# Issuing 334 stores of a hybrid decoder layer from GpSimd's queue instead of SyncE's

## The chip, the cores and the metric

One core of one Trainium2 chip runs one launch of the kernel. The metric is device time in microseconds, the median of several runs. The engines are named as in the profile: PE (TensorE), DVE (VectorE), ACT (ScalarE), POOL (GpSimd) and SP (SyncE, which here does nothing but issue DMAs). All five run their own instruction streams in order and wait for each other through semaphores.

## The reference

One decoder layer in f32, for 1024 prompt tokens and 8 sample tokens (all 1032 columns pass through the same weights). Width 1024.

```
h = LN0(alpha*h + 0.5*swiglu(h; ffn1))
p = h @ w_in                        # RWKV r,k,v and low-rank parts; RG-LRU; GeLU; two gates
rwkv = rwkv7(shifted p, decay, a, gate via low-rank matrices)   # 16 heads x 64, chunked scan
lru  = rg_lru(conv4(p_lru)) * gelu(p_gelu)
h = LN1(alpha*h + (g0*rwkv + g1*lru) @ w_mix_out)
h = LN2(alpha*h + cross_attention(h; 4 heads, 256 memory tokens))
y = LN3(alpha*h + 0.5*swiglu(h; ffn2))
```

It also returns the memory's keys and values (`mk`, `mv`), the RWKV states (`prwkv`, `srwkv`), the last projection columns (`shift`), the last inputs of the convolution (`conv`) and the state of the RG-LRU (`lru`).

## The kernel before, in words

Activations lie transposed: 128 channels on the partitions, 1032 token columns in three chunks of 344 (or four of 256 and one of 8), and eight such blocks `k` for the width. `acc` holds the residual; `HH` and `HL` its high and low parts, since a product is made of three matmuls (`mm3`, L125 to L127: HH x wh, HL x wh, HH x wl). A weight tile of 128x512 is loaded by SP (L94), its high part made by ACT (L99) and its low part by DVE (L100); in the feed-forward parts the same is at L228 and L229, and POOL adds tiles there (L246, L334).

The stages in the order of the trace: feed-forward 1 (0 to 700 us); LN0 and the first columns of the projection (700 to 770); the low-rank part (770 to 880); the mixer (880 to 2000); output projection, LN1 and the memory's keys and values (2000 to 2150); attention (2150 to 2390); LN2 and the start of feed-forward 2 (2390 to 2470); feed-forward 2 with LN3 at its end.

A layer norm (`ln_stream`, L160 to L219) takes one chunk of columns at a time: the mean by a matmul with ones (L169); for each block `k` the subtraction of the mean on DVE (L181), the square on ACT (L183), and for each pair the sum on POOL (L185); the matmuls over the squares on PE (L176); DVE adds epsilon (L192), POOL raises to the power -1/2 (L193), ACT broadcasts (L195), PE transposes (L200); then for each block scale on DVE (L205), bias on ACT (L207), HH on ACT (L214), HL on POOL (L215), and, where the layer norm's result is needed later as a residual, a store of the block to DRAM (L217): `HD` behind LN0 (24 stores of 128x344), `H` behind LN2 (24 of 128x256 and 8 of 128x264).

The mixer writes the projected columns to a DRAM tile `GD`, one for each of eight pairs of heads, and reads them back when their turn comes. `project` (L635) makes one 128-row tile of it: gemm, evacuation on ACT (`ev`, L556), store to GD (L644). That store is issued from POOL for 150 of the 168 tiles, and from SP for the 18 in the low-rank part, where `then` is None. `ends` (L652) copies the last columns of a finished tile from GD to the outputs `shift` (L655) and `conv` (L657): these DMAs go from DRAM to DRAM and wait until the store to GD has landed. The low-rank part stores decay, `a` and gate to GD (L762, L763) and two output columns (L734). Each round of the mixer takes one pair and 256 columns: loads of GD tiles, RWKV chunks on PE, DVE and ACT, the RG-LRU, and the merge. In it, POOL raises to powers for norms (L798 in `inv_norm`, `ivs` and `ivc`, whose results ACT makes into `s` and `gsq` and PE transposes at L804; L1150 and L1220), copies `BN` (L894), and issues loads of `MG` (L1241) and stores of `FD` (L1257). The stores of the rounds are the bonus (L863), the LRU's state and output (L1041, L1046, L1050), the merged rows `MG` (L1084, L1229) and the RWKV states (L1138, L1198). `memory_kv` (L1372) stores each key and value tile twice, to a DRAM tile and to the output (L1396, L1397, L1412). Attention stores the sample queries and probabilities to small DRAM tiles (`qd` L1547, `pd` L1555), which loads read at once.

The program is written as generators that are woven together, and a scheduler then sets the order of each engine's instructions, so a change of an instruction's engine can change the order of others. DMAs are instructions in the stream of the engine that issues them and run in that stream's order. The line at the centre of the change in `project` was:

```
(nc.gpsimd if then else nc.sync).dma_start(out=GD[p][:, gi, c0:c0 + n], in_=e)
```

Of the kernel before, what the change touches and what calls it, by code (L numbers as in the profile page):

```python
# [159 lines left out]
def ln_stream(S, st, li, c0, n, final, keep):  # L160

    nc = S.nc
# [39 lines left out]
    for k in range(KT):  # L202
        d = acc[:, k, c0:c0 + n]
        g, b = S.lng[:, li, k:k + 1], S.lnb[:, li, k:k + 1]
        nc.vector.scalar_tensor_tensor(out=d, in0=d, scalar=g, in1=rs[:, :n], op0=ALU.mult, op1=ALU.mult)  # L205
        if final is None or k % 3 < 2:
            nc.scalar.activation(out=d, in_=d, func=AF.Identity, bias=b)  # L207
        else:
            nc.vector.tensor_scalar(out=d, in0=d, scalar1=b, scalar2=None, op0=ALU.add)  # L209
        if final is not None:  # L210
            nc.sync.dma_start(out=final[128 * k:128 * k + 128, c0:c0 + n], in_=d)
        else:
            hh = S.HH[:, k, c0:c0 + n]
            nc.scalar.activation(out=hh, in_=d, func=AF.Identity)  # L214
            nc.gpsimd.tensor_tensor(out=S.HL[:, k, c0:c0 + n], in0=d, in1=hh.bitcast(F32), op=ALU.subtract)  # L215
            if keep is not None:
                nc.sync.dma_start(out=keep[k, :, c0:c0 + n], in_=d)  # L217
        yield
# [325 lines left out]
def mixer(octx, S, I, O, MG, HD, pre):  # L544
# [13 lines left out]
    with ExitStack() as ctx:  # L558
# [76 lines left out]
        def project(p, mt, gi, func, sc, w, cs, psg, pool, then=None):  # L635

            for c0, n in cs:
                q = psg(n)
                yield from cols(w, c0, n, q)
                if then:  # L640
                    then(c0, n)
                e = pool.tile([128, 344], F32, tag="ev", name="ev", bufs=3 if then else 2)[:, :n]
                ACT(e, q, func, scale=sc)
                (nc.gpsimd if then else nc.sync).dma_start(out=GD[p][:, gi, c0:c0 + n], in_=e)  # L644

# [6 lines left out]
        def ends(p, early):  # L652

            for i in range(3 if early else 0):
                nc.sync.dma_start(out=O["shift"][:, 8 * i + p, :], in_=GD[p][:, i, NP - 1:NT])  # L655
            if not early:
                nc.sync.dma_start(out=O["conv"][:, p, :], in_=GD[p][:, GL, NP - 3:NT])  # L657

# [42 lines left out]
        with ExitStack() as c2:  # L701
# [25 lines left out]
            def low_out():  # L727
                for i in range(2):
# [4 lines left out]
                    STT(x[:, NP:NT], shs[:, 24 + i, :], m1, x[:, NP:NT], ALU.mult, ALU.add)  # L733
                    nc.sync.dma_start(out=O["shift"][:, 24 + i, :], in_=r[:, NP:NT + 1])  # L734
                    if i == 0:
# [7 lines left out]
                for p in range(S.npairs):  # L743
# [6 lines left out]
                    for c0, n in CH3:  # L750
                        t = ep_.tile([128, 3, 344], F32, tag="t", name="t")[:, :, :n]
                        for i, (P_, x) in enumerate(((half[0], 0), (half[1], 0), (slice(0, 128), 1))):
# [7 lines left out]
                            else:  # L760
                                nc.vector.tensor_copy(out=t[:, i], in_=q)
                        nc.sync.dma_start(out=GD[p][:, GZ:GA + 1, c0:c0 + n], in_=t[:, 0:2])  # L762
                        nc.sync.dma_start(out=GD[p][:, GG, c0:c0 + n], in_=t[:, 2])  # L763
                        yield
# [44 lines left out]
        def stage(U, i):  # L809
# [52 lines left out]
            TTo(bv, xv[:, 0:256], pb[:, 0:256], ALU.mult)  # L862
            nc.sync.dma_start(out=GD[p][:, GB, c0:c0 + 256], in_=bv)  # L863
            if n == 0:
# [124 lines left out]
        def branch(p, n, P):  # L989
# [47 lines left out]
            if n == 0:  # L1037
                TTo(hs[:, 256:264], gr[:, 256:264], lst[:, p, :], ALU.mult)
                TTo(hs[:, 256:264], hs[:, 256:264], gi[:, 256:264], ALU.add)
                nc.vector.tensor_copy(out=P.hl, in_=hs[:, 255:264])  # L1040
                nc.sync.dma_start(out=O["lru"][:, p, 1:9], in_=P.hl[:, 1:9])  # L1041
            else:
                nc.vector.tensor_copy(out=P.hl[:, 0:1], in_=hs[:, 255:256])
            P.hl = P.hl[:, 0:1]
            if n == 3:
                nc.sync.dma_start(out=O["lru"][:, p, 0:1], in_=P.hl)  # L1046
            hs = hs[:, :w]
            TTo(hs, hs, ge[:, 0], ALU.mult)
            STT(hs, ge[:, 1], 1.0, hs, ALU.add, ALU.mult)
            nc.sync.dma_start(out=GD[p][:, GM, c0:c0 + 256], in_=hs[:, 0:256])  # L1050
            P.lm.append(n)
# [8 lines left out]
        def post(p, n, Y):  # L1060
# [22 lines left out]
            if p < S.npairs - 2:  # L1083
                nc.sync.dma_start(out=MG[p, :, 256 * n:256 * n + 256], in_=ysb)  # L1084
                ready.add(("mg", p, n))
# [4 lines left out]
        def chain(U, V):  # L1090
# [45 lines left out]
            if n == 3:  # L1136
                for i in range(2):
                    nc.sync.dma_start(out=O["prwkv"][U.p0 + i], in_=sf[:, i])  # L1138
            yield itertools.chain(*(post(U.p0 + i, n, Y[:, 256 * i:256 * i + 256]) for i in range(2))), 14
# [22 lines left out]
        def samples_b(p, P):  # L1162
# [5 lines left out]
            for b0 in (0, 4):  # L1168
# [28 lines left out]
                TTo(s_, s_, r2, ALU.add)  # L1197
                nc.sync.dma_start(out=O["srwkv"][p].rearrange("p (b k) -> p b k", k=64)[:, B], in_=s_)  # L1198
                yield
# [4 lines left out]
        def samples_c(p, P):  # L1204
# [23 lines left out]
            if p < S.npairs - 2:  # L1228
                nc.sync.dma_start(out=MG[p, :, NP:NT], in_=y)  # L1229
                ready.add(("mg", p, 4))  # L1230
# [141 lines left out]
def memory_kv(S, ctx, I, O, psg):  # L1372
# [14 lines left out]
    for m in range(8):  # L1387
# [7 lines left out]
        nc.scalar.activation(out=t, in_=q, func=AF.Identity)  # L1395
        nc.sync.dma_start(out=S.KD[m], in_=t)  # L1396
        nc.sync.dma_start(out=O["mk"][m], in_=t)  # L1397
        yield
    for c in range(4):
# [8 lines left out]
        for i in range(2):  # L1408
            t = pool.tile([128, 256], F32, tag="mi", name="vo")
            nc.scalar.activation(out=t, in_=q[:, i], func=AF.Identity)  # L1410
            for to in (S.VD, O["mv"]):
                nc.sync.dma_start(out=to[i, :, 256 * c:256 * c + 256], in_=t)  # L1412
        yield


def attention(S, I, li, pre, after, keep):
# [3 lines left out]
    with ExitStack() as ctx:  # L1420
# [115 lines left out]
        def samples(h):  # L1536
# [206 lines left out]
```

## Time and profile before

| | us |
|---|---|
| median of 3 runs | 3177.53 |
| lowest and highest | 3172.70 and 3178.56 |
| profiled execution | 3173.59 |
| its span | 3171.8 |

| engine | busy us | share | instructions |
|---|---|---|---|
| PE | 2997.5 | 95% | 23324 |
| DVE | 2196.4 | 69% | 5903 |
| ACT | 1433.0 | 45% | 3193 |
| POOL | 669.7 | 21% | 718 |

The granted clock of PE is 0.971 of full speed on average. The span is the time from the first to the last instruction of one profiled execution; busy time counts what an engine executes, DMAs that POOL issues among it, while SP's work of issuing is not counted as busy. To read it, one goes from the shares to the stages, and there to the waits: each row of a wait tells which engine stood still at which line, for which result of which engine and line.

### The profile page before, as it was taken

To read this page: it belongs to the slowest core of one execution; us is meant where nothing else is said; L and a number is where in the kernel's file an instruction comes from. 1 tells how busy PE (TensorE), PEld (TensorE's weight loads), DVE (VectorE), ACT (ScalarE), POOL (GpSimd) and SP (SyncE) were. 2 spreads that over 40 slices of the span, in tenths; PEclk is the share of its full clock that TensorE was granted. 3 is DMA by queue.
4 is the path that set the end of the run, shared out by engine and by line. 5 is a ranking of instruction groups with operands and counts; after the bars stand their busy time and mean duration, and the time that the engine had idled before them with its cause. 6 is when DMAs were issued, how large, how long until landed. Compare 5 with 4: busy or idle time off the path is not lost. (4 is left out here: it accounts for less than half of the span.)

```text
span 3171.8 us, 63384 instructions
## 1 busy us (share of the span) xinstructions
PE 2997.5 (95%) x23324; PEld 2835.5 (89%) x23324; DVE 2196.4 (69%) x5903; ACT 1433.0 (45%) x3193; POOL 669.7 (21%) x718
## 2 busy tenths in 40 slices
PE   8999999999999999999999989889897999999997
PEld 8999999998888888888887768788897999999997
DVE  7666665564367788877787877666778666666556
ACT  5333342125465565566556655354235333334212
POOL 2222210123021121122112122350005222220111
PEclk9999999999999999999999979799998999999998
DMA  4222243413645555545554454654433222225321
GB/s 139 79 83 78 81 148 109 126 49 110 223 134 137 142 146 145 143 133 144 147 147 131 140 161 131 183 168 134 147 121 121 73 78 81 78 80 161 111 84 54
DMA packets 375943, 386.74 MB, mean 122 GB/s; under 512 B 153904, under 2 KB 267600, under 8 KB 375632
## 3 DMA queue, kind: packets, MB, share of 16 engines
q1 hardware_dynamic: 363344, 348.86, 37.3%
q0 software_dynamic: 12288, 33.83, 3.0%
q8 instruction: 183, 3.00, 0.4%
q14 instruction: 128, 1.05, 0.1%
HBM read 277.54 MB, written 105.23 MB: 121 GB/s over the span
## 5 line engine op out<-in xcount | busy, mean ns | idle before, releaser
L125 PE MATMUL ps<-HH,wh 128*128 128x258 f32 (+1 forms) x2384 | 718.7, 302 | 18.3 <-ACT HH L510 7.4
L126 PE MATMUL ps<-HL,wh 128*128 128x258 f32 (+1 forms) x2384 | 717.1, 301 | 0.6 <-POOL HL L215 0.6
L127 PE MATMUL ps<-HH,wl 128*128 128x258 f32 (+1 forms) x2384 | 715.9, 300 | 0.0
L125 PE MATMUL g<-HH,wh 128*128 128x344 f32 (+2 forms) x1840 | 618.5, 337 | 20.7 <-ACT ev L556 4.5
L127 PE MATMUL g<-HH,wl 128*128 128x344 f32 (+2 forms) x1840 | 596.1, 325 | 2.2 <-DVE wl L100 2.2
L126 PE MATMUL g<-HL,wh 128*128 128x344 f32 (+2 forms) x1840 | 594.1, 323 | 0.5 <-POOL HL L215 0.2
L125 PEld LDWEIGHTS ps<-HH,wh 128*128 128x128 f32 x2384 | 451.4, 189 | 20.7 <-ACT HH L510 7.4
L126 PEld LDWEIGHTS ps<-HL,wh 128*128 128x128 f32 x2384 | 451.2, 189 | 1.4 <-POOL HL L215 0.9
L127 PEld LDWEIGHTS ps<-HH,wl 128*128 128x128 f32 x2384 | 450.6, 189 | 0.0
L125 PEld LDWEIGHTS g<-HH,wh 128*128 128x128 f32 x1840 | 354.5, 193 | 38.1 <-ACT ev L556 6.3
L127 PEld LDWEIGHTS g<-HH,wl 128*128 128x128 f32 x1840 | 354.0, 193 | 7.4 <-DVE wl L100 3.1
L126 PEld LDWEIGHTS g<-HL,wh 128*128 128x128 f32 x1840 | 355.2, 193 | 5.5 <-POOL HL L215 1.4
L334 POOL TENSOR_TENSOR raw<-raw 128x512 f32<-128x512 f32 x160 | 213.8, 1336 | 566.0 <-DVE wl L229 359.0
L228 ACT ACTIVATE wh<-raw 128x512 fp32r<-128x512 f32 x280 | 176.5, 631 | 322.0 <-PE ps L126 260.9
L229 DVE TENSOR_TENSOR wl<-raw,wh 128x512 fp32r<-128x512 f32 x280 | 203.0, 726 | 139.0 <-ACT wh L228 132.1
L99 ACT ACTIVATE wh<-raw 128x512 fp32r<-128x512 f32 x302 | 185.1, 626 | 221.8 <-PE ps L126 77.6
L100 DVE TENSOR_TENSOR wl<-raw,wh 128x512 fp32r<-128x512 f32 x302 | 217.7, 728 | 91.8 <-ACT wh L99 89.4
L442 DVE SCALAR_TENSOR_TENSOR acc<-ps,acc 128x344 f32<-128x344 f32 x336 | 168.4, 512 | 144.2 <-PE ps L127 143.5
L644 POOL DMA_DIRECT2D GD<-ev x150 | 84.4, 563 | 632.5 <-ACT ev L556 411.8
L551 DVE TENSOR_TENSOR pr<-tq,iv 128x2 f32<-128x2 f32 (+30 forms) x496 | 159.7, 322 | 2.8
L556 ACT ACTIVATE ev<-g 128x344 f32<-128x344 f32 x192 | 86.9, 453 | 106.1 <-PE g L127 103.6
L464 POOL TENSOR_TENSOR acc<-acc,raw 128x516 f32<-128x516 f32 x32 | 42.7, 1340 | 420.0 <-DVE acc L442 322.4
(407 smaller groups left out, 6515.5 us busy)
## 6 DMA issues: line engine op xcount, KB each, us to landing
raw<-in_wi_dram SPq DMA_DIRECT2D x176, 256.0 KB
raw<-in_w_in_dram SPq DMA_DIRECT2D x116, 256.0 KB
raw<-in_wo_dram SPq DMA_DIRECT2D x104, 256.0 KB
GD<-ev POOLq DMA_DIRECT2D x150, 172.0 KB, 2.6
raw<-HID SPq DMA_DIRECT2D x88, 258.0 KB
HID<-g SPq DMA_DIRECT2D x80, 258.0 KB
tg<-GD SPq DMA_DIRECT2D x32, 512.0 KB
wt<-T SPq DMA_DIRECT2D x160, 64.0 KB
```

The lines of the kernel that those rows point to most:

```text
L99: nc.scalar.activation(out=hi, in_=raw, func=AF.Identity)
L100: S.low.tensor_tensor(out=lo, in0=raw, in1=hi.bitcast(F32), op=ALU.subtract)
L125: nc.tensor.matmul(ps, wh, xh, start=first, stop=False)
L126: nc.tensor.matmul(ps, wh, xl, start=False, stop=False)
L127: nc.tensor.matmul(ps, wl, xh, start=False, stop=last)
L228: nc.scalar.activation(out=hi, in_=x, func=AF.Identity)
L229: nc.vector.tensor_tensor(out=lo, in0=x, in1=hi.bitcast(F32), op=ALU.subtract)
L334: pool_tt = lambda o, a, b, op: nc.gpsimd.tensor_tensor(out=o, in0=a, in1=b, op=op)
L442: nc.vector.scalar_tensor_tensor(out=a, in0=q, scalar=0.5 / ALPHA, in1=a, op0=ALU.mult, op1=ALU.add)
L551: TTo = lambda o, a, b, op: nc.vector.tensor_tensor(out=o, in0=a, in1=b, op=op)
L556: ACT = lambda o, a, f=AF.Identity, **kw: nc.scalar.activation(out=o, in_=a, func=f, **kw)
L644: (nc.gpsimd if then else nc.sync).dma_start(out=GD[p][:, gi, c0:c0 + n], in_=e)
```

## The change

334 DMAs that SP issued are issued from POOL's queue. Their sources, destinations and shapes stay. By line: L217 56, L644 18, L655 24, L657 8, L734 2, L762 and L763 24 each, L863 32, L1041 8, L1046 8, L1050 32, L1084 24, L1138 8, L1198 16, L1229 6, L1396 and L1397 8 each, L1412 16, L1547 8, L1555 4.

```diff
@@ ln_stream
             if keep is not None:
-                nc.sync.dma_start(out=keep[k, :, c0:c0 + n], in_=d)
+                nc.gpsimd.dma_start(out=keep[k, :, c0:c0 + n], in_=d)
@@ project
-                (nc.gpsimd if then else nc.sync).dma_start(out=GD[p][:, gi, c0:c0 + n], in_=e)
+                nc.gpsimd.dma_start(out=GD[p][:, gi, c0:c0 + n], in_=e)
@@ ends
             for i in range(3 if early else 0):
-                nc.sync.dma_start(out=O["shift"][:, 8 * i + p, :], in_=GD[p][:, i, NP - 1:NT])
+                nc.gpsimd.dma_start(out=O["shift"][:, 8 * i + p, :], in_=GD[p][:, i, NP - 1:NT])
             if not early:
-                nc.sync.dma_start(out=O["conv"][:, p, :], in_=GD[p][:, GL, NP - 3:NT])
+                nc.gpsimd.dma_start(out=O["conv"][:, p, :], in_=GD[p][:, GL, NP - 3:NT])
...
-                        nc.sync.dma_start(out=GD[p][:, GZ:GA + 1, c0:c0 + n], in_=t[:, 0:2])
-                        nc.sync.dma_start(out=GD[p][:, GG, c0:c0 + n], in_=t[:, 2])
+                        nc.gpsimd.dma_start(out=GD[p][:, GZ:GA + 1, c0:c0 + n], in_=t[:, 0:2])
+                        nc.gpsimd.dma_start(out=GD[p][:, GG, c0:c0 + n], in_=t[:, 2])
...
-            nc.sync.dma_start(out=GD[p][:, GB, c0:c0 + 256], in_=bv)
+            nc.gpsimd.dma_start(out=GD[p][:, GB, c0:c0 + 256], in_=bv)
...
-            nc.sync.dma_start(out=GD[p][:, GM, c0:c0 + 256], in_=hs[:, 0:256])
+            nc.gpsimd.dma_start(out=GD[p][:, GM, c0:c0 + 256], in_=hs[:, 0:256])
...
-                nc.sync.dma_start(out=MG[p, :, 256 * n:256 * n + 256], in_=ysb)
+                nc.gpsimd.dma_start(out=MG[p, :, 256 * n:256 * n + 256], in_=ysb)
...
-        nc.sync.dma_start(out=S.KD[m], in_=t)
-        nc.sync.dma_start(out=O["mk"][m], in_=t)
+        nc.gpsimd.dma_start(out=S.KD[m], in_=t)
+        nc.gpsimd.dma_start(out=O["mk"][m], in_=t)
...
-                nc.sync.dma_start(out=to[i, :, 256 * c:256 * c + 256], in_=t)
+                nc.gpsimd.dma_start(out=to[i, :, 256 * c:256 * c + 256], in_=t)
...
-                nc.sync.dma_start(out=qd[:, i], in_=qr[NS * i:NS * i + NS])
+                nc.gpsimd.dma_start(out=qd[:, i], in_=qr[NS * i:NS * i + NS])
...
-            nc.sync.dma_start(out=pd, in_=p)
+            nc.gpsimd.dma_start(out=pd, in_=p)
```

The lines left out (L734, L1041, L1046, L1138, L1198, L1229) are edited in the same way.

POOL's instructions in LN0, from the power of the first chunk to that of the second, before (a row is line, operation, output and input by the program's names, shape, and how many in a row):

```order
L193 TENSOR_TENSOR lnv<-lnv,mhalf 128x3
L215 TENSOR_TENSOR HL<-acc,HH 128x344 x8
L185 TENSOR_TENSOR lnq<-lnq 128x344 x4
L145 TENSOR_TENSOR lns<-lns,acc 128x344
L193 TENSOR_TENSOR lnv<-lnv,mhalf 128x3
```

and after, from behind the chunk's first store to the next chunk's L185:

```order
L215 TENSOR_TENSOR HL<-acc,HH 128x344
L217 DMA HD<-acc 128x344 x2
L215 TENSOR_TENSOR HL<-acc,HH 128x344 x2
L217 DMA HD<-acc 128x344
L215 TENSOR_TENSOR HL<-acc,HH 128x344
L217 DMA HD<-acc 128x344 x2
L215 TENSOR_TENSOR HL<-acc,HH 128x344 x2
L217 DMA HD<-acc 128x344
L215 TENSOR_TENSOR HL<-acc,HH 128x344
L217 DMA HD<-acc 128x344
L215 TENSOR_TENSOR HL<-acc,HH 128x344
L185 TENSOR_TENSOR lnq<-lnq 128x344 x4
```

The eight stores of the chunk (seven of them in these rows) stand among its eight subtractions of L215, all ahead of the next chunk's L185. PE's, DVE's and ACT's orders are the same in this place.

SP's DMAs in the same place, before:

```order
L94 DMA raw<-in_w_in_dram 128x512 x2
L217 DMA HD<-acc 128x344 x8
L94 DMA raw<-in_w_in_dram 128x512 x3
L217 DMA HD<-acc 128x344 x8
L94 DMA raw<-in_w_in_dram 128x512 x7
```

and after:

```order
L94 DMA raw<-in_w_in_dram 128x512 x18
L745 DMA lw<-in_lora_dram 128x256
L94 DMA raw<-in_w_in_dram 128x512 x2
L745 DMA lw<-in_lora_dram 128x256 x2
L94 DMA raw<-in_w_in_dram 128x512
```

The weight loads of L94 now follow each other, with no store among them.

POOL's instructions in the mixer where the 4th pair's tile is finished, before:

```order
L798 TENSOR_TENSOR ivc<-ivc,mhalf 128x4
L644 DMA GD_8807<-ev 128x344 x2
L798 TENSOR_TENSOR ivs<-ivs,mhalf 128x4
L894 COPY BN<-BN 64x4x64
L644 DMA GD_8807<-ev 128x344 x4
L798 TENSOR_TENSOR ivc<-ivc,mhalf 128x4
L798 TENSOR_TENSOR ivs<-ivs,mhalf 128x4
L644 DMA GD_8806<-ev 128x344 x2
L894 COPY BN<-BN 64x4x64
L1220 TENSOR_TENSOR w_13482<-w_13482,mhalf 128x8
```

and after:

```order
L644 DMA GD_8807<-ev 128x344
L655 DMA out_shift_dram<-GD_8807 128x9
L644 DMA GD_8807<-ev 128x344
L1050 DMA GD_8805<-lm 128x256
L644 DMA GD_8807<-ev 128x344 x2
L655 DMA out_shift_dram<-GD_8807 128x9
L798 TENSOR_TENSOR ivc<-ivc,mhalf 128x4
L798 TENSOR_TENSOR ivs<-ivs,mhalf 128x4
L644 DMA GD_8806<-ev 128x344 x2
L863 DMA GD_8806<-bv 128x256
L894 COPY BN<-BN 64x4x64
L1220 TENSOR_TENSOR w_13482<-w_13482,mhalf 128x8
```

Between the same two kinds of computations (powers L798 and L1220, copy L894) stand stores of other rounds, and copies of L655, one of them right ahead of two powers and behind the two GD stores whose landing it needs.

POOL's instructions in LN2's second chunk, before:

```order
L185 TENSOR_TENSOR lnq<-lnq 128x256 x2
L145 TENSOR_TENSOR lns<-lns,acc 128x264
L193 TENSOR_TENSOR lnv<-lnv,mhalf 128x2
L215 TENSOR_TENSOR HL<-acc,HH 128x256 x8
L246 TENSOR_TENSOR acc<-acc 128x258 x2
L185 TENSOR_TENSOR lnq<-lnq 128x264 x2
```

and after:

```order
L145 TENSOR_TENSOR lns<-lns,acc 128x264
L193 TENSOR_TENSOR lnv<-lnv,mhalf 128x2
L217 DMA H_94<-acc 128x256 x2
L215 TENSOR_TENSOR HL<-acc,HH 128x256 x2
L217 DMA H_94<-acc 128x256 x2
L215 TENSOR_TENSOR HL<-acc,HH 128x256 x2
L217 DMA H_94<-acc 128x256 x2
L215 TENSOR_TENSOR HL<-acc,HH 128x256 x2
L217 DMA H_94<-acc 128x256 x2
L215 TENSOR_TENSOR HL<-acc,HH 128x256 x2
L246 TENSOR_TENSOR acc<-acc 128x258 x2
L185 TENSOR_TENSOR lnq<-lnq 128x264 x2
```

Eight stores stand among the eight subtractions ahead of L246 and L185.

## Rows read from the trace of the kernel before

**Rows 1.** The page's first part: busy us of each engine with its share of the span, and its instructions.

```profile
PE 2997.5 (95%) x23324; PEld 2835.5 (89%) x23324; DVE 2196.4 (69%) x5903; ACT 1433.0 (45%) x3193; POOL 669.7 (21%) x718
```

**Rows 2.** Busy time by stage (windows): start:end and length in us, then busy us (and instructions) of PE, PE's weight loads, DVE, ACT and POOL, the granted clock of PE, the DMA engines' share and GB/s. From the top: LN0; the mixer; out projection, LN1 and memory; LN2.

```profile
700.00:770.00 70.00, 63.39 (x386) 60.87 (x386) 37.03 (x75) 38.93 (x87) 36.62 (x38) 0.93 0.33 113
...
880.00:2000.00 1120.00, 1041.89 (x8840) 924.00 (x8840) 867.26 (x2967) 659.07 (x1498) 221.92 (x297) 0.96 0.50 141
2000.00:2150.00 150.00, 132.55 (x1036) 120.97 (x1034) 102.67 (x219) 78.90 (x193) 73.53 (x90) 0.92 0.57 178
...
2390.00:2470.00 80.00, 62.73 (x390) 59.73 (x389) 64.17 (x149) 47.90 (x122) 48.20 (x57) 0.87 0.33 106
```

**Rows 3.** All instructions of L644, a store that the kernel before issues 150 times from POOL and 18 times from SP: instructions, ns min/median/max, first and last start.

```profile
L644 POOL DMA_DIRECT2D GD<-ev x150: 539/542/731, 865.3 to 1846.3; - x150
...
L644 SPq DMA_DIRECT2D GD<-ev x18: 319/326/531, 747.9 to 860.4; - x18
```

**Rows 4.** Time line of POOL in LN0: start us, busy us, line, operation, how many in a row, and in brackets the idle time before with what ended it.

```profile
708.10 6.61 POOL L215 TENSOR_TENSOR HL<-acc,HH 128x344 fp32r<-128x344 f32 x7 [0.40 <-ACT HH L214]
714.68 1.18 POOL L185 TENSOR_TENSOR lnq<-lnq 128x344 f32<-128x344 f32 x1
...
737.25 1.39 POOL L185 TENSOR_TENSOR lnq<-lnq 128x344 f32<-128x344 f32 x1 [0.53 <-PE g L127]
```

**Rows 5.** Time line of PE in LN0, same columns: the matmuls of the squares.

```profile
715.92 0.88 PE L176 MATMUL ln<-ones_d,lnq 128*128 128x64 f32 x6 [1.20 <-POOL lnq L185]
...
738.70 0.88 PE L176 MATMUL ln<-ones_d,lnq 128*128 128x64 f32 x6 [0.56 <-POOL lnq L185]
```

**Rows 6.** Time line of POOL in LN2, same columns.

```profile
2395.30 1.60 POOL L215 TENSOR_TENSOR HL<-acc,HH 128x256 fp32r<-128x256 f32 x2 [0.88 <-ACT HH L214]
2397.26 2.24 POOL L215 TENSOR_TENSOR HL<-acc,HH 128x256 fp32r<-128x256 f32 x3 [0.36 <-ACT HH L214]
2400.77 0.74 POOL L215 TENSOR_TENSOR HL<-acc,HH 128x256 fp32r<-128x256 f32 x1 [1.27 <-ACT HH L214]
2401.87 2.85 POOL L215 TENSOR_TENSOR HL<-acc,HH 128x256 fp32r<-128x256 f32 x4 [0.37 <-ACT HH L214]
2405.95 1.44 POOL L215 TENSOR_TENSOR HL<-acc,HH 128x256 fp32r<-128x256 f32 x2 [1.22 <-ACT HH L214]
2407.95 0.74 POOL L185 TENSOR_TENSOR lnq<-lnq 128x256 f32<-128x256 f32 x1 [0.57 <-POOL HL L215]
...
2425.85 1.70 POOL L246 TENSOR_TENSOR acc<-acc 128x258 f32<-128x258 f32 x2 [0.42 <-POOL HL L215]
2428.16 0.76 POOL L185 TENSOR_TENSOR lnq<-lnq 128x264 f32<-128x264 f32 x1 [0.61 <-ACT lnq L183]
...
2449.02 5.87 POOL L215 TENSOR_TENSOR HL<-acc,HH 128x264 fp32r<-128x264 f32 x7 [3.38 <-ACT HH L214]
```

**Rows 7.** Time line of PE in LN2, same columns.

```profile
2408.75 0.66 PE L176 MATMUL ln<-ones_d,lnq 128*128 128x64 f32 x4
...
2420.37 0.63 PE L125 MATMUL ps<-HH,wh 128*128 128x344 f32 x1 [4.17 <-DVE acc L1576]
...
2430.41 0.78 PE L176 MATMUL ln<-ones_d,lnq 128*128 128x64 f32 x6
...
2456.35 0.42 PE L126 MATMUL ps<-HL,wh 128*128 128x344 f32 x1 [0.60 <-POOL HL L215]
```

**Rows 8.** Windows of 5 us in LN2, columns as in rows 2.

```profile
2415.00:2420.00 5.00, 0.69 (x2) 0.29 (x2) 3.93 (x11) 4.62 (x12) 1.89 (x4) 0.50 0.72 251
2420.00:2425.00 5.00, 4.63 (x16) 4.41 (x17) 5.00 (x7) 3.14 (x10) 5.00 (x6) 0.54 0.74 211
```

**Rows 9.** LN1 and memory: the sum over nine windows of 5 us from 2060 to 2105, and the largest of PE's waits between 2000 and 2150 (line waited at, for what, us in total, times, longest us).

```profile
sum 45.00, PE 39.20 PEld 36.55 DVE 37.07 ACT 29.37 POOL 31.69; mean PE 4.36 PEld 4.06 DVE 4.12 ACT 3.26 POOL 3.52
...
PE ln L176 <- POOL lnq L185: 3.8, 7, 1.0
```

**Rows 10.** PE's waits in the mixer (880 to 2000 us), columns as in the last row.

```profile
PE m L804 <- ACT s L556: 24.6, 12, 3.6
...
PE y L804 <- ACT gsq L556: 7.8, 9, 1.9
```

**Rows 11.** Waits in SP's queue, same columns: the first row at 690 to 770 us, the second in the mixer.

```profile
SPq L217 <- ACT acc L207: 46.7, 14, 33.2
...
SPq L655 <- DMA GD<-ev: 20.0, 8, 5.7
```

**Rows 12.** Waits of ACT and DVE for loads in the mixer, same columns; the last row is from the page's fifth part (line, engine, operation, shapes, count, busy us and mean ns of one, idle before).

```profile
ACT HH L556 <- DMA ev<-MG: 14.7, 8, 6.6
...
ACT wh L99 <- DMA raw<-in_w_in_dram: 7.1, 6, 2.7
...
ACT xc L556 <- DMA cb<-GD: 5.5, 9, 2.1
...
DVE tg L552 <- DMA tg<-GD: 4.1, 4, 1.9
...
L100 DVE TENSOR_TENSOR wl<-raw,wh 128x512 fp32r<-128x512 f32 x302 | 217.7, 728 | 91.8 <-ACT wh L99 89.4
```

**Rows 13.** Time line of POOL in the mixer, columns as in rows 4.

```profile
1683.64 0.60 POOL L644 DMA_DIRECT2D GD<-ev  x1
1684.27 1.67 POOL L1220 TENSOR_TENSOR w<-w,mhalf 128x8 f32<-128x8 f32 x1
```

More of the change, by code (lines that the diff above doesn't have):

```diff
@@ L733, in low_out @@
                     STT(x[:, NP:NT], shs[:, 24 + i, :], m1, x[:, NP:NT], ALU.mult, ALU.add)
-                    nc.sync.dma_start(out=O["shift"][:, 24 + i, :], in_=r[:, NP:NT + 1])
+                    nc.gpsimd.dma_start(out=O["shift"][:, 24 + i, :], in_=r[:, NP:NT + 1])
                     if i == 0:
@@ L1040, in branch @@
                 nc.vector.tensor_copy(out=P.hl, in_=hs[:, 255:264])
-                nc.sync.dma_start(out=O["lru"][:, p, 1:9], in_=P.hl[:, 1:9])
+                nc.gpsimd.dma_start(out=O["lru"][:, p, 1:9], in_=P.hl[:, 1:9])
             else:
@@ L1045, in branch @@
             if n == 3:
-                nc.sync.dma_start(out=O["lru"][:, p, 0:1], in_=P.hl)
+                nc.gpsimd.dma_start(out=O["lru"][:, p, 0:1], in_=P.hl)
             hs = hs[:, :w]
@@ L1137, in chain @@
                 for i in range(2):
-                    nc.sync.dma_start(out=O["prwkv"][U.p0 + i], in_=sf[:, i])
+                    nc.gpsimd.dma_start(out=O["prwkv"][U.p0 + i], in_=sf[:, i])
             yield itertools.chain(*(post(U.p0 + i, n, Y[:, 256 * i:256 * i + 256]) for i in range(2))), 14
@@ L1197, in samples_b @@
                 TTo(s_, s_, r2, ALU.add)
-                nc.sync.dma_start(out=O["srwkv"][p].rearrange("p (b k) -> p b k", k=64)[:, B], in_=s_)
+                nc.gpsimd.dma_start(out=O["srwkv"][p].rearrange("p (b k) -> p b k", k=64)[:, B], in_=s_)
                 yield
@@ L1228, in samples_c @@
             if p < S.npairs - 2:
-                nc.sync.dma_start(out=MG[p, :, NP:NT], in_=y)
+                nc.gpsimd.dma_start(out=MG[p, :, NP:NT], in_=y)
                 ready.add(("mg", p, 4))
```

## The prediction

> **What bounds the kernel now.** First the page's busy shares: PE 2997.5 us of the span, 95%; POOL only 21% [rows 1]. A kernel in this state changes its time where PE is made to wait, or where a wait that PE has is taken away; work put on POOL costs nothing as long as nobody waits for POOL. So the second view is the busy time by stage [rows 2]. The two feed-forward stages, 0 to 700 us and from 2470 us, hold none of the moved stores. In the stages with layer norms POOL is no longer the idle engine: 36.62 of 70 us at 700 to 770, 73.53 of 150 at 2000 to 2150, 48.20 of 80 at 2390 to 2470; in the mixer's 1120 us it is 221.92. The third view is the time line of POOL and of PE in the layer norms [rows 4 to 7], which tells who waits for whom there; the last are the waits of PE, SP, DVE and ACT in the mixer [rows 10 to 12].
>
> Two facts carry everything. A store takes POOL 539 to 731 ns, median 542, where SP spends a median of 326 on it [rows 3]: POOL executes it as an instruction of its own, and what stands behind it waits. One row pair shows this: a store runs on POOL from 1683.64 for 0.60 us, and the power of L1220 starts at 1684.27 with no idle between [rows 13]. I therefore count 0.54 us of POOL for each of 334 stores, 180 us in all, and ask where PE stands behind them.
>
> **LN0, 700 to 770 us (24 stores of L217).** Each of three chunks now puts eight stores among the eight subtractions of L215, ahead of the next chunk's sums of squares (L185). PE's matmuls of the squares wait for L185 at once: 1.20 us at 715.92 and 0.56 us at 738.70 [rows 5]. So POOL is on the path there, without slack. First chunk: 8 x 0.54 = 4.3 us, less the idle of 0.40 us ahead of 708.10 = +3.9. Second: 4.3 less the 0.53 us ahead of 737.25 = +3.8 [rows 4]. The third chunk has no squares behind it, and I cost it at nothing: the low-rank gemms are in front of PE then; without that cover it would be +4. DVE's chain (mean, variance, scale) starts from those matmuls and moves with them, so PE's later waits in this stage don't take the delay back. Sum +7.7, bounds 4 to 12.
>
> **LN2, 2390 to 2470 us (32 stores).** Ahead of the L185 at 2407.95 stand 16 stores: 8.6 us, less POOL's idle gaps of 0.88, 0.36, 1.27, 0.37, 1.22 and 0.57 us = 4.7 [rows 6], leaves +4.0; PE's squares at 2408.75 start 0.06 us after that L185 ends [rows 7]. Ahead of the L185 at 2428.16 stand eight more: 4.3 less gaps of 0.42 and 0.61 us, less the 1.5 us for which its result lies before PE takes it at 2430.41 = +1.8; I take 2. In the last chunk the seven subtractions from 2449.02 are without a gap, and PE waits for the last one, 0.60 us at 2456.35: 7 or 8 stores, +4. Sum +10, bounds 5 to 13. PE's big wait in this stage, 4.17 us until DVE's chain at 2420.37, comes from the same chain of squares and is pushed back whole.
>
> **LN1 and the memory's keys and values (32 stores of L1396, L1397 and L1412).** 32 x 0.54 = 17.3 us more for POOL. Between 2060 and 2105 it is busy 31.69 of 45 us, so 13.3 us are free, and PE waits for its squares seven times in the stage [rows 9]. What doesn't fit is 17.3 - 13.3 = +4; bounds 0 (all of it in gaps) and 17 (none). I take 4, because the gaps lie between the chains, not in them, but not all stores fall into this stretch.
>
> **The clock.** After a stretch in which PE mostly waited, 2415 to 2420 with 0.69 us of work, the granted clock is 0.50 and then 0.54 of full speed, the lower of the two levels (1.2 of 2.4 GHz) [rows 8]. Five us at half speed cost about 2.4 us of matmul. I have five or six new stalls of 2 to 4 us; some of them only lengthen a stall that already has its slow stretch. Half of 6 x 2.4 = +7, bounds 0 and 14.
>
> **Mixer and low-rank part.** Some 234 stores come here, 126 us on top of POOL's 222 in 1120. POOL's urgent work is short: the 62 powers of L798 and 16 others, about 78. PE waits for their followers, 24.6 us in 12 waits for `s` and 7.8 us in 9 for `gsq` [rows 10], so roughly a third of them have no slack. A power that meets a store (10% of the time) waits 0.27 us on average: 78 x 0.10 x 0.27 = 2 us. Then L655 and L657: 32 stores whose source is written by a store just issued, which must land first; on SP this wait is 2.5 us where it shows (20.0 us in 8) [rows 11]. Now POOL stands still in it, 32 x 2.5 = 80 us, 7% of the stage: 78 x 0.07 x 1.25 = another 7 us on powers. A third to all of these 9 us reaches PE: I take +5. Upper bound: 11 of the 32 stand one or two places ahead of a power in the new order, each at the full 2.5 us, +28. Lower bound 0. The stores with sources of DVE stand in POOL's order behind computations that need DVE's earlier results anyway, so a wait for DVE at POOL's head costs nothing that I can see.
>
> **What SP gives back.** SP no longer stands before stores with loads behind it: 46.7 us of waits of L217 at 690 to 770, 20.0 of L655 [rows 11]. But who waits for loads? In the mixer ACT and DVE, 14.7 + 7.1 + 5.5 + 4.1 = 31.4 us in the largest rows [rows 12], and most of that lies beside PE's work; the first, the largest, is a load on POOL's own queue of data that moved stores write. Bounds 0 and -26, taken -3. The scheduler also writes the order of all engines in the mixer anew, since stores have another engine; that can go either way and is in the range. **Attention:** 12 stores that a load reads at once, each some 0.2 us longer to issue: +1, bounds 0 and 4.
>
> The Trainium skill, "DMA: Bandwidth & Descriptors", section "Issuing engines are not separate DMA queues", says that issuing from several engines saves only the issuing sequencer's time. By it SP's relief is issue time that no row here shows PE waiting on, so 0 in place of -3, and the sum below would be 3 us higher.
>
> **The sum.** 7.7 + 10 + 4 + 7 + 5 - 3 + 1 = +31.7 us. The profiled execution took 3173.59 us (span 3171.8), and the median of the runs is 3177.53, 4 us above it. On the profiled run this makes 3205.3, on the median 3209.2; I give 3207, between the two.
>
> **The rivals.** (A) *Faster.* The freed SP queue brings tiles earlier and the new order closes half of PE's idle time in the mixer, 1120 - 1041.89 = 78 us [rows 2], so -39: 3207 - 39 = 3168. It decides from about 32 us won there. For it: SP's waits before stores are long. Against: the loads that are waited for sum to 31 us, off PE. Chance 0.11.
> (B) *No change.* PE's delays are taken back by waits that come anyway (4.17 and 0.60 us [rows 7]) and by SP's relief: within 6 us of 3177. Against: those waits hang on the same chains. Chance 0.12.
> (C) *Stores on POOL starve beside DVE.* As a mechanism of this kernel: a store would be held until DVE's running instruction ends, up to 0.73 us (the mean of DVE's splits of L100 [rows 12]), on the 40 stores of the norm chains: +29, so 3236. The 150 stores that POOL issues already run beside a DVE that is busy 867.26 of 1120 us [rows 2] and last 731 ns at most [rows 3], which speaks against it. Chance 0.05. This is the rule of the Trainium skill, "SBUF — State Buffer", section "SBUF: two separate sides": descriptors of a GpSimd DMA can't be written while DVE holds the shared port in a two-port mode, about 620 against 3100 ns; by that rule, the trace disagrees for the stores that it has.
> (D) *The landing waits reach PE.* The upper bound of +28 in the mixer in place of +5: 3207 + 23 = 3230 and more. Decides if powers stand behind L655 when `s` is awaited. Chance 0.10.
>
> **How the numbers follow.** Forecast 0.62, between 3190 and 3225; C and D 0.15 above; B 0.12; A 0.11. What this kernel's measurement can tell from no change is about 0.2%, 6.4 us. Slower 0.62 + 0.05 + 0.10 = 0.77, same 0.12, faster 0.11. The range leaves out the far half of A and the worst of C and D: 3173 to 3240.
>
> **What would show it.** Right: PE's waits for L185 grow by about 4 us each at two places of LN0 and two or three of LN2; POOL's rows there read L215, L217, L215; POOL's busy time rises by some 180 us to 850; the two feed-forward stages keep their length; slow-clock stretches follow the new stalls. Wrong: if PE idles less in the mixer by over 30 us (A), if the squares start no later (the store is cheaper behind L215 than alone, B), if stores on POOL exceed 1 us (C), or if the wait for `s` doubles from 24.6 us (D).

## The result and the profile after

The changed kernel takes 3200.64 us (median of 4 runs, 3197.72 to 3207.86) against 3178.05 us of the kernel before in the same comparison: a ratio of 1.0075, 95% interval 1.0053 to 1.0098, some 23 us slower. The forecast was 3207 us on a range of 3173 to 3240. The profiled execution has a span of 3195.9 us, 24.1 more than before.

The page's first part of the kernel after, busy us of each engine:

```profile
PE 3000.2 (94%) x23324; PEld 2844.9 (89%) x23324; DVE 2213.6 (69%) x5903; ACT 1431.8 (45%) x3193; POOL 843.1 (26%) x1052
```

Against [rows 1] POOL has 173 us more, 334 instructions at 0.52 us, and PE has the same work, 2.7 us longer. PE's idle time is what grew: 3195.9 - 3000.2 = 195.7 us in place of 3171.8 - 2997.5 = 174.3. So the question is where PE stands still for 21 us more.

The windows of LN0, of the mixer and of LN2 in the kernel after, columns as in [rows 2]; each window is moved and widened with the program's delay at its ends:

```profile
700.00:778.00 78.00, 64.93 (x366) 62.30 (x366) 38.55 (x71) 39.10 (x87) 49.67 (x65) 0.87 0.28 98
...
888.00:2010.00 1122.00, 1037.03 (x8859) 925.72 (x8858) 876.23 (x2978) 661.14 (x1504) 300.60 (x456) 0.96 0.50 141
2407.00:2495.00 88.00, 65.70 (x373) 61.80 (x374) 64.87 (x142) 47.96 (x123) 59.66 (x84) 0.83 0.29 96
```

POOL is now busy 49.67 of 78 us in LN0 and 59.66 of 88 in LN2. In the mixer it has 79 us more, and PE's busy time there stays within 5 us.

To lay the delay on the stages, one takes an instruction that stands at the same place of both programs. The powers L193 of the layer norms serve: the first and third chunk of LN0, and the first and last of those of LN2 shown here. Time line of POOL before:

```profile
702.84 0.87 POOL L193 TENSOR_TENSOR lnv<-lnv,mhalf 128x3 f32<-128x3 f32 x1
...
750.19 0.86 POOL L193 TENSOR_TENSOR lnv<-lnv,mhalf 128x3 f32<-128x3 f32 x1 [4.78 <-DVE lnv L192]
...
2383.09 0.89 POOL L193 TENSOR_TENSOR lnv<-lnv,mhalf 128x2 f32<-128x2 f32 x1
...
2444.77 0.86 POOL L193 TENSOR_TENSOR lnv<-lnv,mhalf 128x3 f32<-128x3 f32 x1 [1.21 <-DVE lnv L192]
```

and after:

```profile
700.37 0.87 POOL L193 TENSOR_TENSOR lnv<-lnv,mhalf 128x3 f32<-128x3 f32 x1
...
758.55 0.87 POOL L193 TENSOR_TENSOR lnv<-lnv,mhalf 128x3 f32<-128x3 f32 x1 [1.44 <-DVE lnv L192]
...
2395.53 0.90 POOL L193 TENSOR_TENSOR lnv<-lnv,mhalf 128x2 f32<-128x2 f32 x1
...
2464.70 0.87 POOL L193 TENSOR_TENSOR lnv<-lnv,mhalf 128x3 f32<-128x3 f32 x1 [1.88 <-DVE lnv L192]
```

LN0 from its first to its third power takes 47.35 us before and 58.18 after: +10.8. From there to LN2 (low-rank part, mixer, LN1, memory, attention) it is 1632.90 and 1636.98: +4.1. Between LN2's powers 61.68 and 69.17: +7.5. What stands ahead of the first power was 2.5 us earlier in this execution, with the same instructions, and from the last power to the end another 4.2 us come, of which 2.4 are LN2's last chunk (from the power to the last instruction of L319, at 2481.6 before and 2503.9 after). Of these steps LN0's and LN2's stand out of what differs from one execution to the next: with the norm stores on SP, the two stretches between powers last 45.79 to 47.35 and 61.68 to 62.81 us in the traces of this document, and with them ahead of the squares 56.35 us and more and 69.17 us and more. The +4.1 between them does not: in the traces of five experiments below with the same 278 other stores on POOL that stretch lasts 1634.84 to 1649.77 us.

In LN0, time line of POOL after, the end of the first chunk's subtractions:

```profile
713.47 0.92 POOL L215 TENSOR_TENSOR HL<-acc,HH 128x344 fp32r<-128x344 f32 x1
714.32 0.56 POOL L217 DMA_DIRECT2D HD<-acc  x1
714.91 0.92 POOL L215 TENSOR_TENSOR HL<-acc,HH 128x344 fp32r<-128x344 f32 x1
715.79 0.91 POOL L185 TENSOR_TENSOR lnq<-lnq 128x344 f32<-128x344 f32 x1
```

and PE's squares behind them, time line of PE after:

```profile
716.75 1.54 PE L176 MATMUL ln<-ones_d,lnq 128*128 128x64 f32 x6 [4.11 <-POOL lnq L185]
...
744.05 1.54 PE L176 MATMUL ln<-ones_d,lnq 128*128 128x64 f32 x6 [3.80 <-POOL lnq L185]
```

The pair to be seen is the wait in brackets: 4.11 and 3.80 us for L185, where [rows 5] have 1.20 and 0.56. Stores and subtractions fill POOL without a gap, and L185, at 715.79, begins the moment they end. What these two waits have grown by is 6.1 us of the 10.8. Most of the rest is the clock: the same six matmuls take 1.54 us in place of 0.88, and the windows of 5 us of the kernel after (columns as before) show why:

```profile
715.00:720.00 5.00, 3.25 (x14) 3.26 (x14) 1.44 (x5) 1.36 (x3) 3.33 (x4) 0.65 0.10 35
720.00:725.00 5.00, 5.00 (x26) 5.00 (x26) 1.32 (x3) 0.87 (x2) 1.99 (x3) 0.67 0.00 0
745.00:750.00 5.00, 5.00 (x19) 5.00 (x19) 3.02 (x4) 1.96 (x5) 1.57 (x2) 0.50 0.36 111
```

The granted clock is 0.65 and 0.67 on average in the two windows at the first stall and 0.50 behind the second; 0.50 is the lower of the two levels (1.2 of 2.4 GHz). In the second and third of these windows PE is busy for all 5 us.

How much is waiting and how much is slow matmuls is seen in windows that begin and end at the same two matmuls in both kernels, columns as before. LN0 and LN2 before:

```profile
702.13:760.04 57.91, 51.30 (x306) 48.78 (x306) 36.19 (x72) 34.20 (x77) 31.43 (x33) 0.91 0.34 113
2380.00:2480.02 100.02, 82.53 (x531) 79.06 (x530) 77.86 (x187) 56.55 (x143) 52.89 (x62) 0.90 0.33 106
```

and after:

```profile
699.67:768.38 68.71, 55.64 (x307) 53.01 (x306) 38.69 (x72) 34.37 (x77) 41.85 (x54) 0.85 0.27 93
2392.31:2502.33 110.02, 86.67 (x531) 82.10 (x530) 82.18 (x187) 56.20 (x143) 67.16 (x94) 0.86 0.30 96
```

LN0 takes 10.8 us more and LN2 10.0. In LN0 PE stands still 6.5 us longer (length less busy time, 13.07 in place of 6.61) and needs 4.3 us more for the same matmuls; in LN2 it is 5.9 us (23.35 in place of 17.49) and 4.1. The granted clock falls from 0.91 to 0.85 and from 0.90 to 0.86.

LN2, time line of POOL after:

```profile
2424.21 1.09 POOL L217 DMA_DIRECT2D H<-acc  x2
2425.32 0.73 POOL L185 TENSOR_TENSOR lnq<-lnq 128x256 f32<-128x256 f32 x1
...
2447.09 0.79 POOL L185 TENSOR_TENSOR lnq<-lnq 128x264 f32<-128x264 f32 x1 [0.45 <-ACT lnq L183]
```

and of PE:

```profile
2426.11 0.75 PE L176 MATMUL ln<-ones_d,lnq 128*128 128x64 f32 x4 [3.48 <-POOL lnq L185]
...
2438.10 0.62 PE L125 MATMUL ps<-HH,wh 128*128 128x344 f32 x1 [5.08 <-DVE acc L1576]
```

The squares of the chunk wait 3.48 us, where [rows 7] show none; DVE's chain then makes PE wait 5.08 us in place of 4.17, so the delay was not taken back. The second place that I had counted, L185 at 2447.09, makes no wait at all. The 2.4 us of the last chunk are hardly a wait either: from the transposes behind its power (2446.24 before, 2466.19 after) to the end of the windows above PE stands still 2.68 us in place of 2.45, and its matmuls take 33.46 us in place of 31.33, at a granted clock of 0.89 in place of 0.92.

### The profile page after: what moved, and what is told of

Its sections match the earlier page's. It is cut to its first block, busy times and chain, and to the rows that moved or that the text cites. A ratio compares the mean times of both kernels' runs of the same rounds, so it can differ in the third digit from the quotient of the medians.

```text
span 3195.9 us, 63566 instructions
## 1 busy us (share of the span) xinstructions
PE 3000.2 (94%) x23324; PEld 2844.9 (89%) x23324; DVE 2213.6 (69%) x5903; ACT 1431.8 (45%) x3193; POOL 843.1 (26%) x1052
## 3 DMA queue, kind: packets, MB, share of 16 engines
q1 hardware_dynamic: 313712, 306.15, 33.2%
## 5 line engine op out<-in xcount | busy, mean ns | idle before, releaser
L229 DVE TENSOR_TENSOR wl<-raw,wh 128x512 fp32r<-128x512 f32 x280 | 205.5, 735 | 136.5 <-ACT wh L228 129.3
L100 DVE TENSOR_TENSOR wl<-raw,wh 128x512 fp32r<-128x512 f32 x302 | 226.3, 756 | 101.0 <-ACT wh L99 97.6
L644 POOL DMA_DIRECT2D GD<-ev x168 | 93.3, 555 | 383.8 <-ACT ev L556 333.1
```

The lines of the kernel that those rows point to most:

```text
L100: S.low.tensor_tensor(out=lo, in0=raw, in1=hi.bitcast(F32), op=ALU.subtract)
L229: nc.vector.tensor_tensor(out=lo, in0=x, in1=hi.bitcast(F32), op=ALU.subtract)
L644: nc.gpsimd.dma_start(out=GD[p][:, gi, c0:c0 + n], in_=e)
```

## The experiments

Each time is the median of 5 to 12 executions, and each ratio is against the kernel before, run beside it on the same chip, with its 95% interval. That kernel's median was 3180.93 us beside the first two experiments and those on the memory's stores and the copies, 3181.33 beside the third to the sixth, and 3176.27 beside the last; so the ratios are what can be compared.

**The norm stores back on SP.**

```diff
-                nc.gpsimd.dma_start(out=keep[k, :, c0:c0 + n], in_=d)
+                nc.sync.dma_start(out=keep[k, :, c0:c0 + n], in_=d)
```

> The changed kernel with only the 56 stores of L217 given back to SP; the other 278 moved stores stay on POOL. Theory (the layer-norm stores carry the loss: against the kernel before the trace of the changed one is 13.7 us later over LN0 and the low-rank part, 0 over the mixer, 1 over LN1 to attention, 10 over LN2): 3180 us, between 3176 and 3186. Rival (the mixer's stores and their landing waits cost PE time that the stage offsets only hide, or the low-rank part's stores do): 3190 or more.

Measured: 3184.85 us, ratio 1.0012 (1.0002 to 1.0022). 278 of the 334 stores stay on POOL and cost about 4 us together (0.6 to 7 by the interval). PE's time line in LN0 of this run reads as before the change:

```profile
715.54 0.88 PE L176 MATMUL ln<-ones_d,lnq 128*128 128x64 f32 x6 [1.22 <-POOL lnq L185]
...
736.77 0.88 PE L176 MATMUL ln<-ones_d,lnq 128*128 128x64 f32 x6 [0.38 <-POOL lnq L185]
```

**The norm stores alone**, the mirror image: the kernel before with the opposite edit on that one line.

> The kernel before with only the 56 stores of L217 moved to POOL. Theory: nearly the whole loss, 3195 to 3202 us. Rival (half of it is from the low-rank part's stores or the rewritten order): 3188 or less.

Measured: 3202.53 us, ratio 1.0073 (1.0059 to 1.0086). 56 of 334 stores carry what all of them cost, as forecast (the time itself is half a microsecond above the range). Between the matmuls of the windows above, LN0 takes 68.01 us in this run's trace and LN2 113.32. The two runs agree with each other, so a rewritten order of the mixer plays no large part.

**LN0's stores on POOL, LN2's on SP.**

```diff
-                nc.gpsimd.dma_start(out=keep[k, :, c0:c0 + n], in_=d)
+                (nc.sync if li else nc.gpsimd).dma_start(out=keep[k, :, c0:c0 + n], in_=d)
```

> The changed kernel with only LN2's 32 stores given back to SP. Theory (each norm's stores cost by themselves, LN0 about 11 us and LN2 about 10): halfway between the changed kernel and the run with all norm stores on SP, 1.004 to 1.0055 of the kernel before, some 3193 to 3198 us. Rival (one of the norms carries it all): 1.001 or 1.0075.

Measured: 3196.0 us, ratio 1.0050 (1.0032 to 1.0068). LN0's stores cost 1.0050 - 1.0012, 12 us; LN2's the rest up to 1.0075, 8 us; the intervals leave 6 to 9 us of doubt on each. The trace is plainer: between the same matmuls LN0 takes 66.88 us, 9.0 more than before, and LN2 100.54, 0.5 more. Both count, as the rows above say (10.8 and 10.0).

**LN0's stores held back.** The eight stores of a chunk stay on POOL, but an order edge puts them behind the next chunk's last L185 (the last chunk's stay where they are, and LN2's are on SP):

```diff
+    if li == 0:
+        store_held(S, last)          # last: the chunk's fourth L185
     yield
     squares(KT - 1)
...
-            if keep is not None:
-                nc.gpsimd.dma_start(out=keep[k, :, c0:c0 + n], in_=d)
+            if keep is not None and li:
+                nc.sync.dma_start(out=keep[k, :, c0:c0 + n], in_=d)
+            elif keep is not None:
+                S.held.append((keep[k, :, c0:c0 + n], d))
```

> LN2's stores on SP, and LN0's 24 stores on POOL as in the changed kernel, but each chunk's eight held back until the next chunk's L185 have been issued (an order edge, no wait for data). Theory of position (a store costs only because squares stand behind it on POOL): most of LN0's 11 us is gone, 1.001 to 1.0025, some 3184 to 3188 us; about 1 us stays, because the power L193 then stands behind eight stores. Rival (POOL's time for a store costs wherever it stands, or the transfer of a POOL store disturbs): as with LN0 on POOL, 1.004 to 1.0055.

Measured: 3179.71 us, ratio 0.9998 (0.9985 to 1.0010). The same stores on the same queue cost nothing that the times show when no squares stand behind them, less even than the 1.001 that was expected at least. Time line of POOL in this run (its L163 is the store L217, its L204 the power L193):

```profile
720.73 4.51 POOL L163 DMA_DIRECT2D HD<-acc  x8
725.25 0.89 POOL L204 TENSOR_TENSOR lnv<-lnv,mhalf 128x3 f32<-128x3 f32 x1
```

and of PE (its L185 is the matmul L176, its L194 POOL's sum L185):

```profile
715.87 0.88 PE L185 MATMUL ln<-ones_d,lnq 128*128 128x64 f32 x6 [1.20 <-POOL lnq L194]
...
744.68 1.09 PE L185 MATMUL ln<-ones_d,lnq 128*128 128x64 f32 x6 [2.24 <-POOL lnq L194]
```

and the window of LN0 between the same two matmuls as above:

```profile
702.09:762.03 59.94, 52.62 (x306) 49.76 (x306) 36.99 (x72) 33.00 (x74) 41.40 (x51) 0.91 0.32 104
```

Eight stores run in one row of 4.51 us, partly in what was POOL's idle time ahead of the power, and PE's first squares wait 1.20 us as in [rows 5]. The power stands behind them and starts when they end. This is not quite free: the second squares wait 2.24 us in place of 0.56, and LN0 takes 59.94 us against 57.91 before and 68.71 after the change. So 2.0 of the 10.8 us stay in this one execution, below what the times can tell.

**The norm stores halved**: each of the 56 in two of half the columns, the same bytes in twice as many instructions.

```diff
-                nc.gpsimd.dma_start(out=keep[k, :, c0:c0 + n], in_=d)
+                for x, y in ((c0, c0 + n // 2), (c0 + n // 2, c0 + n)):
+                    nc.gpsimd.dma_start(out=keep[k, :, x:y], in_=acc[:, k, x:y])
```

> The changed kernel with each of the 56 norm stores cut into two of half the columns: twice as many issues on POOL, the same bytes. Theory (POOL's issue time, 0.54 us a store whatever its size): the norm stores' loss of some 20 us grows by 14 to 22, 1.012 to 1.0145, some 3218 to 3226 us. Rival (the bytes or the landing matter): no change, 1.0075.

Measured: 3214.28 us, ratio 1.0109 (1.0088 to 1.0130). More instructions cost more, 11 us more than the change, but less than the 14 expected at least. Rows of this run: the stores (L218) with min/median/max ns, and PE's squares in LN0:

```profile
L218 POOL DMA_DIRECT2D H<-acc x64: 537/555/616, 2411.9 to 2499.7; - x64
L218 POOL DMA_DIRECT2D HD<-acc x48: 539/542/730, 706.0 to 786.6; - x48
...
723.06 1.54 PE L176 MATMUL ln<-ones_d,lnq 128*128 128x64 f32 x6 [5.44 <-POOL lnq L185]
...
751.99 1.54 PE L176 MATMUL ln<-ones_d,lnq 128*128 128x64 f32 x6 [5.80 <-POOL lnq L185]
```

A store of half the size takes POOL as long, 542 and 555 ns at the median, so POOL's time did double. The waits grew to 5.44 and 5.80 us from 4.11 and 3.80, by 1.3 and 2.0, where the change itself had added 2.9 and 3.2. The windows between the same matmuls say where: LN2 grows by 10.2 us over the change (110.02 to 120.22), as much again as by the first dose, and LN0 by 4.6 (68.71 to 73.27), less than half of it. Why LN0 meets less of the second dose was not tried; what is certain is that the loss goes with the count of instructions and not with the bytes.

**POOL's work in place of the stores.** The stores are on SP; ahead of each subtraction of a norm that stores, its first 180 columns are subtracted once more. It adds computation and leaves out none:

```diff
+            if keep is not None:
+                nc.gpsimd.tensor_tensor(out=S.HL[:, k, c0:c0 + 180], in0=d[:, 0:180], in1=hh[:, 0:180].bitcast(F32),
+                                        op=ALU.subtract)
             nc.gpsimd.tensor_tensor(out=S.HL[:, k, c0:c0 + n], in0=d, in1=hh.bitcast(F32), op=ALU.subtract)
             if keep is not None:
-                nc.gpsimd.dma_start(out=keep[k, :, c0:c0 + n], in_=d)
+                nc.sync.dma_start(out=keep[k, :, c0:c0 + n], in_=d)
```

> The norm stores on SP, and in their place on POOL a computation of about the same length: ahead of each of the 56 subtractions of L215 its first 180 columns are subtracted once more (about 0.55 us by the rows of 128x256 and 128x344). Theory (only POOL's time ahead of the squares counts, not that it is a DMA): as the changed kernel, 1.006 to 1.0085, some 3199 to 3207 us. Rival (stores from POOL cost as DMAs, by their landing or by SP's absence): near the run with norm stores on SP, 1.001 to 1.003.

Measured: 3208.35 us, ratio 1.0092 (1.0074 to 1.0109). Rows of this run: the added computation, and PE's squares in LN0:

```profile
L216 POOL TENSOR_TENSOR HL<-acc,HH x56: 552/578/1032, 706.7 to 2485.7; 128x180 fp32r<-128x180 f32 x56
...
720.91 1.54 PE L176 MATMUL ln<-ones_d,lnq 128*128 128x64 f32 x6 [6.44 <-POOL lnq L185]
...
750.20 1.54 PE L176 MATMUL ln<-ones_d,lnq 128*128 128x64 f32 x6 [5.52 <-POOL lnq L185]
```

A computation of 578 ns in the store's place costs PE as much, even a little more than the range said (6.44 and 5.52 us of waits). Two things would make it more, neither tried by itself: it waits for HH where a store needs only the bias before it, and some of its rows last 0.84 to 1.03 us in LN0. So POOL's time ahead of the squares is enough for the whole loss, without a DMA and its landing.

**The memory's stores back on SP** (L1396, L1397, L1412: `nc.gpsimd` to `nc.sync`, the rest as changed).

> The changed kernel with the 32 stores of keys and values (L1396, L1397, L1412) given back to SP. By the prediction's sum they cost 4 us: 3197 us. By the stage offsets, LN1 is up to 8 us later but attention gives 6 of it back: 3199 to 3201. A rival by which LN1's last chunk sets the end: 3193.

Measured: 3201.44 us, ratio 1.0069 (1.0056 to 1.0082). Not to be told from the change's 1.0075. The 4 us that I charged are not seen in the time, and the intervals don't exclude them. The stage itself shows more. Its first and last powers before:

```profile
2058.34 1.19 POOL L193 TENSOR_TENSOR lnv<-lnv,mhalf 128x2 f32<-128x2 f32 x1
...
2130.97 0.86 POOL L193 TENSOR_TENSOR lnv<-lnv,mhalf 128x3 f32<-128x3 f32 x1 [3.12 <-DVE lnv L192]
```

and after the change:

```profile
2067.70 1.11 POOL L193 TENSOR_TENSOR lnv<-lnv,mhalf 128x2 f32<-128x2 f32 x1
...
2149.89 1.27 POOL L193 TENSOR_TENSOR lnv<-lnv,mhalf 128x3 f32<-128x3 f32 x1 [4.57 <-DVE lnv L192]
```

From one to the other it is 72.63 us before, 82.19 after, and 77.60 in this run: LN1 did get 9.6 us longer, and giving these stores back takes 4.6 of it away. But from there to LN2's first power it is 252.12, 245.64 and 247.72 us, so the attention stage gives most of it back.

**The copies of L655 and L657 back on SP** (`nc.gpsimd` to `nc.sync`, the rest as changed).

> The changed kernel with the 32 copies of L655 and L657 given back to SP, so that POOL no longer stands in the 45 us of waits for landing (33.0 of L655, 12.2 of L657). By the prediction's term most of 5 us comes back: 3196 to 3198 us. Theory that PE has slack there, since the mixer's length did not change: 3199 to 3202.

Measured: 3204.36 us, ratio 1.0084 (1.0068 to 1.0101). No gain that can be told; the waits at POOL's head don't reach PE. The rows of the kernel after: PE's waits in the mixer, and what POOL stood idle for ahead of L655 and of L657 (us, times):

```profile
PE m L804 <- ACT s L556: 22.3, 12, 3.3
...
PE y L804 <- ACT gsq L556: 10.9, 7, 2.8
...
  DMA GD<-ev: 33.0, 19
...
  DMA GD<-ev: 12.2, 6
```

POOL stood 33.0 + 12.2 us waiting for landings, and PE's waits for `s` and `gsq` are 22.3 + 10.9 = 33.2 us against 24.6 + 7.8 = 32.4 in [rows 10]. The powers themselves did come later. ACT's waits for the power behind `gsq` in the mixer, before, after, and in this run:

```profile
ACT gsq L556 <- POOL ivc L798: 48.4, 23, 4.3
...
ACT gsq L556 <- POOL ivc L798: 65.2, 26, 4.7
...
ACT gsq L556 <- POOL ivc L798: 49.5, 21, 4.3
```

They grew by 16.8 us and are back with the copies on SP, but the time is not: what ACT waits for here, PE has slack for.

**Half of the subtractions on DVE**, in the other direction: the kernel before, stores on SP, with POOL relieved in LN0 and LN2.

```diff
-            nc.gpsimd.tensor_tensor(out=S.HL[:, k, c0:c0 + n], in0=d, in1=hh.bitcast(F32), op=ALU.subtract)
+            (nc.vector if li != 1 and k % 2 else nc.gpsimd).tensor_tensor(out=S.HL[:, k, c0:c0 + n], in0=d, in1=hh.bitcast(F32), op=ALU.subtract)
```

> The kernel before (stores on SP) with the subtractions L215 of odd blocks made by DVE in LN0 and LN2, so that POOL has four less per chunk. Theory (POOL's queue ahead of the squares is on PE's path already in the kernel before, but only by the waits it shows: 1.8 us in LN0 and the short ones of LN2): a gain of 2 to 5 us with the slow clock behind those stalls, ratio 0.998 to 0.9995. Rival (the waits pass on to ACT's squares and DVE's chain, which gets four subtractions more per chunk): no gain or a loss, 0.9995 to 1.002.

Measured: 3181.81 us, ratio 1.0019 (1.0006 to 1.0033), a loss, within what the rival gave. PE's time line in LN0 of this run:

```profile
715.52 0.88 PE L176 MATMUL ln<-ones_d,lnq 128*128 128x64 f32 x6 [0.21 <-POOL lnq L185]
...
739.44 0.88 PE L176 MATMUL ln<-ones_d,lnq 128*128 128x64 f32 x6 [2.08 <-POOL lnq L185]
```

The first wait falls from 1.20 to 0.21 us, and the second grows from 0.56 to 2.08, now that DVE subtracts between its own steps of the norm. Between the same matmuls LN0 takes 56.32 us, 1.6 less than before, and LN2 100.23 against 100.02. So the relief won a little in LN0 of this trace, and the loss in the time came from elsewhere; where is not shown.

## Why the prediction was right

**The mechanism.** Stores ahead of L185 on POOL make PE's squares late, and carry nearly all of the loss: shown four ways, by undoing it (1.0012), by doing it alone (1.0073), by holding the same stores back (0.9998), and by putting a computation in their place (1.0092). The rival that stores starve beside DVE is out: the median norm store took 557 ns and the longest 730, in the rows of the kernel after (min/median/max ns):

```profile
L217 POOL DMA_DIRECT2D H<-acc x32: 539/557/617, 2404.2 to 2476.9; - x32
L217 POOL DMA_DIRECT2D HD<-acc x24: 539/557/730, 704.0 to 773.1; - x24
...
L762 POOL DMA_DIRECT2D GD<-t x24: 715/715/734, 799.5 to 868.6; - x24
```

The prediction took 0.73 us, the mean of DVE's splits, for the longest hold, and a mean is no upper bound; the rows decide without it. The Trainium skill ("SBUF — State Buffer", section "SBUF: two separate sides") has a DMA of GpSimd at about 3100 ns when DVE holds the shared port in a two-port mode. Beside DVE's 876.23 busy us in the mixer and its splits in the norms no store of these lines came near that. But no row here shows whether DVE was ever in such a mode, so the case neither bears that rule out nor contradicts it; the prediction said too much in calling it a disagreement.

**LN0, 7.7 us.** The two waits grew by 6.1, PE's idle time in the stage by 6.5, and with the slow matmuls it is 10.8. The two places are right, and so is the delay on POOL: behind the chunk's power L185 starts 3.6 and 3.8 us later than before, for +3.9 and +3.8. PE's waits grew by less, 2.9 and 3.2, because L185 then took 0.91 and 0.90 us in place of 1.18 and 1.39 and, in the first chunk, because PE came to the squares 0.4 us later itself.

**LN2, 10 us.** This term was for waits alone, and PE's idle time in the stage grew by 5.9: it is the term that was most too large, by 4. The first chunk gave 3.5 of wait for 4.0. The second place gave none for 2: PE's squares there start without idle time before them. In the last chunk PE's idle time grew by 0.2 for 4. That the whole stage came out at 10.0 us, the figure of the term, is chance: slow matmuls made up what the waits lacked.

**The clock, 7 us.** The same matmuls took 4.3 us more in LN0 and 4.1 in LN2, 8.5 in all, so the size is about right. The way to it was not: I counted six stalls as new where the trace has two in LN0 and one in LN2. Over the whole span PE's busy time grew by 2.7 us only; between LN0's window and LN2's, where the order is a new one, it fell from 1501.60 to 1495.54 us.

**Mixer, LN1, memory and attention, +5 - 3 + 4 + 1.** Between the two windows, from 760.04 to 2380.00 us before and from 768.38 to 2392.31 after, it is 4.0 us more for the 7 that were forecast, and 278 stores cost about 4 in the runs; the traces above scatter by more than that. Which part of it is the memory's, the landing waits' or the new order's stays open: each alone is below what the times can tell. The step that failed is the passing on of late powers: POOL stood 45 us for landings, not 80, and ACT waited 16.8 us longer for one kind of power, more than the 9 that I had for all, yet PE's waits behind the powers grew by 0.8 and not by a third or more of it. The relief of SP is seen where I looked for it, and was worth nothing that shows there: ACT's wait for tiles of w_in, 7.1 us in [rows 12], is no longer among its largest waits in the mixer, and PE's waits are no shorter for it. The memory's 4 us are there in LN1, as the powers of that stage show, and are mostly gone again before LN2; PE's waits for squares in the stage even fell, from 3.8 us in [rows 9] to 2.0.

The sum of +31.7 us stands against a span that is 24.1 longer: 10.8, 4.0 and 10.0 in the three stretches, and 0.7 less for what lies outside them, where no store was moved. The forecast was high because of LN2's waits (4.1 too much), the stretch between the norms (3.0) and LN0's waits (1.2), and low by 1.5 in the clock. The mechanism that carried the result is the forecast one: a wait of PE for the very instruction that would be late, with the slow clock behind it. A delay on POOL or ACT without such a wait was worth little.

## What to carry to other kernels

An engine that is 21% busy over the span can be the one that PE waits for in a stage of 70 us; before giving it work, read the stage, and look for an instruction of that engine that another waits for with no slack. A store moved to POOL's queue costs its time there, 0.54 to 0.72 us at the median here, and what matters is what stands behind it: the same stores cost some 10 us ahead of LN0's squares and about 2 behind them. To tell a wait from a slow clock, measure both kernels between the same two instructions of the engine. SP's queue looked crowded, with long waits before its stores, yet relieving it won nothing that can be told: relief of a queue is worth only what the consumers' waits for it show.

## What the runs showed that I had not expected

POOL's time for a store hardly depends on its size: 542 ns for 128x172 and 557 for 128x344 at the median, and 715 ns for 128x2x344; so one store for two blocks would by estimate cost 715 where two cost 1114, which no run tried. The same code ahead of the first change differed by 2.5 us between two executions, and the slower clock behind stalls of 4 us (0.50 to 0.67 in the windows above) added 4.3 us to 6.1 us of waits in LN0.
